# Weight squares of layer 1 taken during layer 0's merges, from a second load of each tile

## The chip, the cores and the metric

The kernel runs on one core of a Trainium2 chip. The metric is the device time of one execution in microseconds (us). The engines have their own instruction streams and meet by semaphores: TensorE (PE) multiplies matrices, VectorE (DVE), ScalarE (ACT) and GpSimd (POOL) work on tiles in on-chip memory, SyncE (SP) mostly issues loads. On each engine, and in SyncE's queue, instructions run in the order of the program.

## The reference

Two blocks run one after the other on 512 tokens of width 1024, in float32. The first (one layer: spatial gating, a sparse attention, a cross attention, a feed-forward part) is untouched. The second has two layers; each mixes 512 latent tokens and 256 context tokens by three branches (windowed attention a, latent attention b, gated convolution c), gates each branch's output and adds them up:

```
parts = split(h @ w_in, IN_SIZES)   # q,k,v; latents; conv b,c,u; z and g of each branch
ya, yb, yc = window_attention, latent_attention, gated_convolution
m = sigmoid(ga)*(ya @ w_branch[0]) + sigmoid(gb)*(yb @ w_branch[1]) + sigmoid(gc)*(yc @ w_branch[2])
x = x + gate * rms_norm(m @ w_o)
```

Layer 0 works on all 768 columns, layer 1 needs only the 512 latent ones at its end. `w_in` and `w_branch` differ by layer.

## The kernel before

Every float32 product is three float16 (or, for some weights, fp32r) matmuls of halves: hi x hi, lo x hi and hi x lo (lines 416 to 418). The weights' halves are made on the fly by the class `Stream`. It loads chunks of 128x1024 floats (512 KB) from SyncE's queue (line 205) into one of nine raw slots, in the order in which the products use them; makes a hi half `wh` on ScalarE (line 273) or, for convolution, latent and some gate weights, on GpSimd (line 271); and a lo half `wl` on VectorE (line 291, in pieces of 512 columns). Up to nine converted units stand in a ring ahead of TensorE. Once a chunk's lo half is made, its raw slot is free and `freed` issues the next load.

float16 halves need a scale. A group of chunks (the weights of one product, or of a gate and its branch) shares one, from the sum of all its squares. `stat` takes the squares of a raw chunk on ScalarE with a running sum along the row (line 224); the squared values go to the lo tile as scratch, and only the sum is kept. `scale` calls `total` (lines 427 to 433): a reduction on VectorE, a sum over the partitions on TensorE, a power on GpSimd, a reciprocal on VectorE. Only then can the group's halves be made. `stat` runs up to `AHEAD` = 4 chunks ahead of the conversion.

The scheduler of the framework fixes each engine's order before the launch, from its own times; the program only says in which order work is offered. The stage that matters are the twelve `merge` calls of each layer (three branches n, four column groups f2). A merge computes a gate tile (tanh on ScalarE, line 2129, named z) and a branch tile, and VectorE multiplies and adds them (lines 2133 to 2137). Products go through a pool of three PSUM tiles, `mm`. Behind the merges come the output product with `w_o` (fp32r, no squares), the residual chains (lines 2185 to 2206) with their norms, and the start of layer 1: keys and queries (L1556, L1586, L1589), whose transposed inputs are hTh and hTl (lines 421, 422), then attention with its probabilities P (line 721).

Of the kernel before, what the change touches and what calls it, by code (L numbers as in the profile page):

```python
# [9 lines left out]
FT = mybir.dt.float32  # L10
# [113 lines left out]
class Group:  # L124


    def __init__(self):
        self.total = self.seen = self.cols = 0
        self.t = None
        self.ready = False  # L130
        self.made = {}


class Blk:
# [42 lines left out]

G_S, G_I, G_C = 8, 9, 10  # L180


class Stream:
    def __init__(self, nc, slots, ringp, scalep, total, state, blks):
        self.nc, self.slots, self.ringp, self.scalep = nc, slots, ringp, scalep
        self.total, self.state = total, state
        self.chunks = [c for b in blks for c in b.chunks]
        self.units = []
        for ci, (_, us) in enumerate(self.chunks):
            for u in us:  # L190
                self.units.append((ci, u))
        self.raw = {}
        self.nd = 0
        self.ns = 0
        self.nstat = 0
        self.live = 0
        self.full = []
        self.half = None

    def loads(self):  # L200
        while self.nd < len(self.chunks) and self.slots:
# [7 lines left out]

    def stat(self, lo):  # L210
        nc = self.nc
        us = self.chunks[self.nstat][1]
        t = self.raw[self.nstat]
        self.nstat += 1
        g = us[0].blk.grp
        if g is None:
            return False
        if g.t is None:
            g.t = self.scalep.tile([128, 16], FT, tag="gs", name="gs")
        m = sum(len(u.ks) for u in us) * us[0].n  # L220
        w = lo.shape[-1]
        for a in range(0, m, w):
            b = min(m, a + w)
            nc.scalar.activation(lo[:, :b - a], t[:, a:b], AF.Square, accum_out=g.t[:, g.cols:g.cols + 1])  # L224
            g.cols += 1
        g.seen += 1
        if g.seen == g.total:
            self.full.append((self.state.clk, g))
        return True


    def scale(self):
        _, g = self.full.pop(0)
        self.total(g.t[:, 0:g.cols], g.t[:, G_S:G_S + 1], g.t[:, G_I:G_I + 1])
        g.ready = True

    def pump(self, must=False):
        self.loads()
        while self.full and self.full[0][0] + LAG <= self.state.clk:
            self.scale()  # L240
        if self.ns >= len(self.units) or self.live >= RING:
            self.finish()
            return False
        nc = self.nc
        ci, u = self.units[self.ns]
        t = self.raw[ci]
        fr = u.blk.fr
        g = u.blk.grp
        if not (must or fr or g.ready) and g.seen == g.total:
            return False  # L250
        hi, lo = (self.ringp.tile([128, 512 if fr else 1024], FR if fr else F16, tag=n, name=n) for n in ("wh", "wl"))
        if not fr:
            while g.seen < g.total:
                self.stat(lo)
            while not g.ready:
                self.scale()
        n = 1 if self.ns < 4 else 2
        while n and self.nstat < self.nd and self.nstat <= ci + AHEAD:
            n -= self.stat(lo)
        m = len(u.ks) * u.n  # L260
        src = t[:, u.off:u.off + m]
        self.finish()
        if u.blk.split is not None:
            u.blk.split(t, hi, lo)
        elif fr:
            nc.scalar.activation(hi[:, :m], src, AF.Copy)  # L266
            nc.vector.tensor_sub(lo[:, :m], src, hi[:, :m].bitcast(FT))  # L267
        else:
            s = g.t[:, G_S:G_S + 1]
            if u.blk.pool:  # L270
                nc.gpsimd.tensor_scalar(hi[:, :m], src, s, 1.0, op0=OP.mult, op1=OP.mult)  # L271
            else:
                nc.scalar.activation(hi[:, :m], src, AF.Copy, scale=s)  # L273
            self.half = lo[:, :m], src, s, hi[:, :m], ci, u
        u.hi, u.lo, u.split = hi, lo, True
        self.live += 1
        self.ns += 1
        if fr:
            u.ready = True
            if u.last:  # L280
                self.freed(ci)
        return True
# [10 lines left out]
            self.freed(ci)  # L293

    def freed(self, ci):
        self.slots.append(self.raw.pop(ci))
        self.loads()


    def unscale(self, blk, ih, mul=1.0):  # L300
        if blk.fr:
            return None
        while not blk.grp.ready:
            assert self.pump(True), "the weights cannot be read ahead"
        made = blk.grp.made
        key = id(ih), mul
        if key not in made:
            a = G_C + len(made)
            assert a < 16
            c = blk.grp.t[:, a:a + 1]  # L310
            self.nc.vector.tensor_scalar(c, blk.grp.t[:, G_I:G_I + 1], ih, mul, op0=OP.mult, op1=OP.mult)
            made[key] = c, ih
        return made[key][0]

# [17 lines left out]
def decoder_kernel(ctx: ExitStack, tc: tile.TileContext, A: dict, out: bass.AP):  # L332
# [14 lines left out]
    sp = pool("small", NS)  # L347
    s1p = pool("small2", NS2)
    dnp = pool("dn", 3)
    scalep = pool("scales", 12)  # L350
    sbp = pool("sb", 4)
    XN = lambda *a, **k: rot["xn"](*a, **k)
    Z = lambda *a, **k: rot["z"](*a, **k)
# [219 lines left out]
    H = {p: Halves(*[one.tile([128, 4, 512], FR, tag=f"H{p}{i}", name=f"hT{p}") for i in range(2)]) for p in "hl"}  # L573

    def hT16():
        for i, p in enumerate("hl"):
            H[p] = one.tile([128, 8, 512], F16, tag=f"H{p}0", name=f"hT{p}")
            more_raw(f"H{p}1")

    def more_raw(tag):  # L580
        t = one.tile([128, 2, 1024], FT, tag=tag, name="raw")
        stream.slots += [t[:, 0], t[:, 1]]
        stream.loads()
# [1649 lines left out]
    def layer(i):  # L2233
# [3 lines left out]
        every = [4, 5, 0, 1, 2, 3]  # L2237
        qt = every if i == 0 else [0, 1, 2, 3]
        nn = 768 if i == 0 else 512
        add(lambda: s23_start(i))  # L2240
        add(lambda b: form_a(b, every, hcx, ev_ka, f"l{i}"), wblk(w[:, KA:KA + 256]))
        add(lambda b: form_a(b, qt, hcx, ev_qa, f"l{i}", 0.125), wblk(w[:, QA:QA + 512]))
# [37 lines left out]
        for n, b in enumerate((2, 0, 1)):  # L2280
            if n == 0:
                add(lambda: yc_load(nn))
                for n2 in range(behind, len(pieces)):
                    f, sg = pieces[n2]
                    add(lambda *b, n2=n2: piece(n2), *([za[f]] if sg == segs[0] else []))
                add(lambda: ya_load(nn))
            elif n == 1:
                g = Group()
                for f2 in range(2):
                    add(lambda bl, f2=f2: zgate(f2, segs, bl, yb_d, nn),  # L2290
                        wblk(w[:, ZB + f2 * 256:ZB + (f2 + 1) * 256], g))
            for f2 in range(4):
                g = Group()
                add(lambda *bl, f2=f2, n=n, b=b: merge(f2, segs, bl, n == 0, n == 2, "cab"[n]),
                    wblk(w[:, GA + b * 1024 + f2 * 256:GA + b * 1024 + (f2 + 1) * 256], g),
                    wblk(A["w_branch_2"][i, b][:, f2 * 256:(f2 + 1) * 256], g))
        add(lambda: wo_start(i, nq))
        wo = A["w_o_2"][i]
        add(lambda b: form_a(b, qt, mA, wo0), wblk(wo[:, 0:512], fr=True))
# [145 lines left out]
```

## Time and profile before

| | |
|---|---|
| median of 3 runs | 2428.55 us (2423.89 to 2429.85) |
| profiled execution | 2421.47 us, span 2419.7 us |
| mean granted clock | 0.978 |
| TensorE busy | 2261.3 us, 93% of the span |
| VectorE, ScalarE, GpSimd | 1544.2, 1298.1, 320.7 us (64%, 54%, 13%) |
| loads and stores | 226.67 MB, mean 94 GB/s |
| squares, line 224 | 242, 222.9 us |

The profile is of one execution, the page's times add up to its span, and its time lies at the low end of the runs. Busy shares are averages over the whole span; the stretches of the table in the rows below differ a lot. Layer 0's merges run from about 1391 to 1565 us and beyond, with the output product behind them until about 1726; then the norms and the start of layer 1 until about 1770; layer 1's attention and convolution until about 2170; and its merges and output product to the end.

### The profile page before, as it was taken

The page shows a single profiled execution, that of the slowest core. Times are in us where ns is not written, and L with a number is a line of the kernel's source. Part 1 is how long each engine was busy: PE and PEld are TensorE (multiplying, and loading weights), DVE is VectorE, ACT ScalarE, POOL GpSimd, SP SyncE. Part 2 cuts the span into 40 slices and gives each one's busy share as a digit, 9 for nine tenths or more (in the row PEclk, how much of TensorE's full clock was granted, in tenths as well). Part 3 has the DMA queues.
Part 4 walks back from the last instruction along what each step waited for, and adds up shares of the span by engine and source line. Part 5 has one row for each costly group of instructions (what it writes and reads, how often), then busy time and mean ns, then how long its engine had stood idle before and what let it go on. Part 6 is the DMA issues. An engine that isn't in the chain of part 4 may idle for free. (4 is left out here: it accounts for less than half of the span.)

```text
span 2419.7 us, 38066 instructions
## 1 busy us (share of the span) xinstructions
PE 2261.3 (93%) x14342; PEld 1505.2 (62%) x14342; DVE 1544.2 (64%) x3136; ACT 1298.1 (54%) x2745; POOL 320.7 (13%) x703
## 2 busy tenths in 40 slices
PE   7899899899999989999988999999779999899998
PEld 6777687544444557767767566557546567764446
DVE  6878678656665677665777444443777657865543
ACT  5656457746655455535777434323535457775532
POOL 4320321100100211004000000000621121000001
PEclk9899899899999999999999999999989999999999
DMA  4512445534443411112221422211421113233311
GB/s 158 140 47 71 141 144 199 172 101 153 155 140 106 122 50 38 46 40 65 79 74 56 137 79 61 79 42 63 156 86 50 42 38 108 71 115 113 103 44 61
DMA packets 182220, 226.67 MB, mean 94 GB/s; under 512 B 28556, under 2 KB 130876, under 8 KB 182036
## 3 DMA queue, kind: packets, MB, share of 16 engines
q1 hardware_dynamic: 158084, 187.67, 25.1%
q10 hardware_dynamic: 23952, 36.57, 4.4%
q8 instruction: 112, 1.84, 0.3%
q14 instruction: 72, 0.59, 0.1%
HBM read 207.33 MB, written 16.88 MB: 93 GB/s over the span
## 5 line engine op out<-in xcount | busy, mean ns | idle before, releaser
L416 PE MATMUL mm<-hTh,wh 128*128 128x512 f16 (+1 forms) x1040 | 392.6, 378 | 7.3 <-ACT wh L273 3.1
L291 DVE SCALAR_TENSOR_TENSOR wl<-raw,gs,wh 128x512 f16<-128x512 f32 (+2 forms) x420 | 296.6, 751 | 150.6 <-ACT wl L224 116.5
L417 PE MATMUL mm<-hTl,wh 128*128 128x512 f16 (+1 forms) x1040 | 392.4, 377 | 0.0
L418 PE MATMUL mm<-hTh,wl 128*128 128x512 f16 (+1 forms) x1040 | 391.2, 377 | 0.0
L224 ACT ACTIVATE wl<-raw 128x1024 f16<-128x1024 f32 (+3 forms) x242 | 222.9, 921 | 69.6 <-PE mm L417 37.3
L416 PEld LDWEIGHTS <-wh 128*128 128x128 f16 x1712 | 168.0, 98 | 147.4 <-issue 6.8
L417 PEld LDWEIGHTS <-wh 128*128 128x128 f16 x1712 | 168.0, 98 | 146.1 <-issue 9.6
L418 PEld LDWEIGHTS <-wl 128*128 128x128 f16 x1712 | 167.8, 98 | 143.9 <-issue 0.6
L738 ACT ACTIVATE ph<-mm 128x512 f16<-128x512 f32 (+2 forms) x300 | 146.1, 502 | 162.4 <-PE mm L734 156.1
L273 ACT ACTIVATE wh<-raw,gs 128x1024 f16<-128x1024 f32 x156 | 175.3, 1141 | 105.9 <-PE mm L417 83.0
L266 ACT ACTIVATE wh<-raw 128x512 fp32r<-128x512 f32 (+2 forms) x244 | 141.7, 613 | 142.2 <-PE mm L418 49.7
L739 DVE SCALAR_TENSOR_TENSOR pl<-mm,ph 128x512 f16<-128x512 f32 (+2 forms) x300 | 165.9, 567 | 73.6 <-ACT ph L738 71.1
L267 DVE TENSOR_TENSOR wl<-raw,wh 128x512 fp32r<-128x512 f32 (+2 forms) x244 | 156.1, 667 | 55.3 <-ACT wh L266 40.2
L432 POOL TENSOR_TENSOR gs<-gs,nh 128x1 f32<-128x1 f32 x66 | 40.6, 616 | 1125.2 <-DVE gs L431 1079.3
L416 PE MATMUL mm<-wh,hTh 128*128 128x512 f32 (+5 forms) x512 | 181.7, 356 | 5.5 <-DVE vf L1589 2.0
L418 PE MATMUL mm<-wh,hTl 128*128 128x512 f32 (+5 forms) x512 | 180.1, 352 | 1.8 <-DVE hTl L422 1.7
L417 PE MATMUL mm<-wl,hTh 128*128 128x512 f32 (+5 forms) x512 | 180.1, 352 | 0.3 <-DVE wl L267 0.3
L734 PE MATMUL mm<-ident,P 128*128 128x128 f32 x928 | 153.9, 283 | 5.9 <-ACT P L721 2.0
L721 ACT ACTIVATE P<-S,s 128x768 f32<-128x768 f32 (+4 forms) x160 | 105.8, 666 | 35.1 <-PE mm L734 18.0
L734 PEld LDWEIGHTS mm<-ident,P 128*128 128x128 f32 x928 | 108.6, 145 | 19.6 <-ACT P L721 2.9
L2133 DVE SCALAR_TENSOR_TENSOR z<-z,mm 128x256 f32<-128x256 f32 (+1 forms) x72 | 42.8, 596 | 107.2 <-PE mm L418 98.9
L271 POOL TENSOR_SCALAR wh<-raw,gs 128x1024 f16<-128x1024 f32 (+3 forms) x54 | 65.8, 1219 | 328.2 <-PE mm L417 209.9
(503 smaller groups left out, 5360.8 us busy)
## 6 DMA issues: line engine op xcount, KB each, us to landing
raw<-in_w_in_dram SPq DMA_DIRECT2D x124, 512.0 KB, 3.5
raw<-in_w_ff_dram SPq DMA_DIRECT2D x64, 512.0 KB, 4.5
raw<-in_w_mod_dram SPq DMA_DIRECT2D x48, 512.0 KB, 5.1
raw<-in_w_branch_dram SPq DMA_DIRECT2D x24, 512.0 KB, 3.4
raw<-in_w_o_dram SPq DMA_DIRECT2D x16, 512.0 KB, 4.0
raw<-in_cmp_w_dram SPq DMA_DIRECT2D x16, 256.0 KB, 3.5
raw<-in_w_out_dram SPq DMA_DIRECT2D x8, 512.0 KB, 3.6
raw<-in_w_mkv_dram SPq DMA_DIRECT2D x8, 512.0 KB, 3.7
```

The source lines that it names most:

```text
L224: nc.scalar.activation(lo[:, :b - a], t[:, a:b], AF.Square, accum_out=g.t[:, g.cols:g.cols + 1])
L266: nc.scalar.activation(hi[:, :m], src, AF.Copy)
L267: nc.vector.tensor_sub(lo[:, :m], src, hi[:, :m].bitcast(FT))
L273: nc.scalar.activation(hi[:, :m], src, AF.Copy, scale=s)
L291: self.nc.vector.scalar_tensor_tensor(l[:, b], src[:, b], s, h[:, b], op0=OP.mult, op1=OP.subtract)
L416: PE.matmul(ps, ah, bh, start=start, stop=False)
L417: PE.matmul(ps, ah, bl, start=False, stop=False)
L418: PE.matmul(ps, al, bh, start=False, stop=stop)
L721: ACT.activation(P, v[:, j, :], AF.Exp, bias=it.nb[:, j:j + 1], accum_out=it.den[:, j:j + 1])
L734: PE.transpose(ps[:, a - a0, :], it.P[0 if len(it.P) == 1 else j][:, c:c + 128], ident)
L738: ACT.activation(ph[:, :m], ps[:, :m], AF.Copy, scale=PSC)
L739: DVE.scalar_tensor_tensor(pl[:, :m], ps[:, :m], PSC, ph[:, :m], op0=OP.mult, op1=OP.subtract)
```

## The change

At layer 0's merge (n = 0, f2 = 1) the next raw slot that comes free is kept (`keep`, `slot`) and not given back to the stream. From then on, each time the stream is pumped, `early_step` may issue one extra load of a chunk of layer 1 into that slot (line 263), and the step after it takes the chunk's squares in place on ScalarE (line 276), with the sums in a small tile `gse` of 14 groups. When all are done the slot goes back. The 39 chunks are layer 1's first key and query weights (2 and 4), convolution (16), latent (3 and 4) and za gate weights (4), and the weights of its first two merges (6): some 20 MB loaded twice. The regular load of each stays; its squares (line 224, now 234) don't: `stat` passes over the chunks in `seen`. On ScalarE 49 squares of layer 1 (22 of 1024 columns, 20 of 512, 7 between) give way to 39 in layer 0's merges. The pool of scale tiles goes from 12 buffers to 6. Until the first early load each engine has the same instructions in the same order.

```diff
--- before.py
+++ after.py
@@ -129,6 +129,7 @@
         self.t = None
         self.ready = False
         self.made = {}
+        self.at = 8, 9, 10, 16
 
 
 class Blk:
@@ -177,7 +178,8 @@
 
 
 
-G_S, G_I, G_C = 8, 9, 10
+
+EARLY = 4, 5, 6, 8
 
 
 class Stream:
@@ -196,6 +198,10 @@
         self.live = 0
         self.full = []
         self.half = None
+        self.index = {id(c): i for i, c in enumerate(self.chunks)}
+        self.jobs, self.job, self.seen = [], None, set()
+        self.every = self.next = 0.0
+        self.slot, self.keep = None, False
 
     def loads(self):
         while self.nd < len(self.chunks) and self.slots:
@@ -209,12 +215,16 @@
 
     def stat(self, lo):
         nc = self.nc
-        us = self.chunks[self.nstat][1]
-        t = self.raw[self.nstat]
+        i = self.nstat
+        us = self.chunks[i][1]
+        t = self.raw[i]
         self.nstat += 1
         g = us[0].blk.grp
-        if g is None:
+        if g is None or i in self.seen:
             return False
+        if i == self.job:
+            self.early_sum()
+            return True
         if g.t is None:
             g.t = self.scalep.tile([128, 16], FT, tag="gs", name="gs")
         m = sum(len(u.ks) for u in us) * us[0].n
@@ -223,19 +233,67 @@
             b = min(m, a + w)
             nc.scalar.activation(lo[:, :b - a], t[:, a:b], AF.Square, accum_out=g.t[:, g.cols:g.cols + 1])
             g.cols += 1
+        g.cols -= 1
+        self.counted(g)
+        return True
+
+
+    def early(self, blks, tile, every):
+        grps = []
+        for b in blks:
+            if b.grp not in grps:
+                grps.append(b.grp)
+            self.jobs += [self.index[id(c)] for c in b.chunks]
+        n = EARLY[3]
+        for i, g in enumerate(grps):
+            assert g.t is None
+            g.t, g.at = tile[:, i * n:(i + 1) * n], EARLY
+        self.every, self.next = every, self.state.clk
+        self.keep = True
+
+    def early_step(self):
+        if self.slot is None or self.state.clk < self.next:
+            return
+        if self.job is not None:
+            self.early_sum()
+        while self.jobs:
+            i = self.jobs.pop(0)
+            if i >= self.nd:
+                for dst, src in self.chunks[i][0]:
+                    self.nc.sync.dma_start(out=dst(self.slot), in_=src)
+                self.job = i
+                break
+        if self.job is None:
+            self.slots.append(self.slot)
+            self.slot = None
+        self.next = self.state.clk + self.every
+
+    def early_sum(self):
+        us = self.chunks[self.job][1]
+        g = us[0].blk.grp
+        m = sum(len(u.ks) for u in us) * us[0].n
+        t = self.slot[:, :m]
+        self.nc.scalar.activation(t, t, AF.Square, accum_out=g.t[:, g.cols:g.cols + 1])
+        self.seen.add(self.job)
+        self.job = None
+        self.counted(g)
+
+    def counted(self, g):
+        g.cols += 1
         g.seen += 1
         if g.seen == g.total:
             self.full.append((self.state.clk, g))
-        return True
 
 
     def scale(self):
         _, g = self.full.pop(0)
-        self.total(g.t[:, 0:g.cols], g.t[:, G_S:G_S + 1], g.t[:, G_I:G_I + 1])
+        a = g.at
+        self.total(g.t[:, 0:g.cols], g.t[:, a[0]:a[0] + 1], g.t[:, a[1]:a[1] + 1])
         g.ready = True
 
     def pump(self, must=False):
         self.loads()
+        self.early_step()
         while self.full and self.full[0][0] + LAG <= self.state.clk:
             self.scale()
         if self.ns >= len(self.units) or self.live >= RING:
@@ -266,7 +324,7 @@
             nc.scalar.activation(hi[:, :m], src, AF.Copy)
             nc.vector.tensor_sub(lo[:, :m], src, hi[:, :m].bitcast(FT))
         else:
-            s = g.t[:, G_S:G_S + 1]
+            s = g.t[:, g.at[0]:g.at[0] + 1]
             if u.blk.pool:
                 nc.gpsimd.tensor_scalar(hi[:, :m], src, s, 1.0, op0=OP.mult, op1=OP.mult)
             else:
@@ -293,8 +351,12 @@
             self.freed(ci)
 
     def freed(self, ci):
-        self.slots.append(self.raw.pop(ci))
-        self.loads()
+        t = self.raw.pop(ci)
+        if self.keep:
+            self.slot, self.keep = t, False
+        else:
+            self.slots.append(t)
+            self.loads()
 
 
     def unscale(self, blk, ih, mul=1.0):
@@ -305,10 +367,11 @@
         made = blk.grp.made
         key = id(ih), mul
         if key not in made:
-            a = G_C + len(made)
-            assert a < 16
+            g = blk.grp
+            a = g.at[2] + len(made)
+            assert a < g.at[3]
             c = blk.grp.t[:, a:a + 1]
-            self.nc.vector.tensor_scalar(c, blk.grp.t[:, G_I:G_I + 1], ih, mul, op0=OP.mult, op1=OP.mult)
+            self.nc.vector.tensor_scalar(c, g.t[:, g.at[1]:g.at[1] + 1], ih, mul, op0=OP.mult, op1=OP.mult)
             made[key] = c, ih
         return made[key][0]
 
@@ -347,7 +410,7 @@
     sp = pool("small", NS)
     s1p = pool("small2", NS2)
     dnp = pool("dn", 3)
-    scalep = pool("scales", 12)
+    scalep = pool("scales", 6)
     sbp = pool("sb", 4)
     XN = lambda *a, **k: rot["xn"](*a, **k)
     Z = lambda *a, **k: rot["z"](*a, **k)
@@ -573,9 +636,12 @@
     H = {p: Halves(*[one.tile([128, 4, 512], FR, tag=f"H{p}{i}", name=f"hT{p}") for i in range(2)]) for p in "hl"}
 
     def hT16():
-        for i, p in enumerate("hl"):
+        for p in "hl":
             H[p] = one.tile([128, 8, 512], F16, tag=f"H{p}0", name=f"hT{p}")
             more_raw(f"H{p}1")
+
+    early = {}
+    gse = one.tile([128, 14 * EARLY[3]], FT, tag="gse", name="gse")
 
     def more_raw(tag):
         t = one.tile([128, 2, 1024], FT, tag=tag, name="raw")
@@ -2237,6 +2303,7 @@
         every = [4, 5, 0, 1, 2, 3]
         qt = every if i == 0 else [0, 1, 2, 3]
         nn = 768 if i == 0 else 512
+        n0 = len(ops)
         add(lambda: s23_start(i))
         add(lambda b: form_a(b, every, hcx, ev_ka, f"l{i}"), wblk(w[:, KA:KA + 256]))
         add(lambda b: form_a(b, qt, hcx, ev_qa, f"l{i}", 0.125), wblk(w[:, QA:QA + 512]))
@@ -2294,6 +2361,10 @@
                 add(lambda *bl, f2=f2, n=n, b=b: merge(f2, segs, bl, n == 0, n == 2, "cab"[n]),
                     wblk(w[:, GA + b * 1024 + f2 * 256:GA + b * 1024 + (f2 + 1) * 256], g),
                     wblk(A["w_branch_2"][i, b][:, f2 * 256:(f2 + 1) * 256], g))
+                if i == 0 and (n, f2) == (0, 1):
+                    add(lambda: stream.early(early[1], gse, 8000))
+                elif (n, f2) == (0, 1):
+                    early[i] = [b for blks, _ in ops[n0:] for b in blks if not b.fr]
         add(lambda: wo_start(i, nq))
         wo = A["w_o_2"][i]
         add(lambda b: form_a(b, qt, mA, wo0), wblk(wo[:, 0:512], fr=True))
```

The places where instructions move are shown as they stand in each engine's order. In the changed kernel's numbering, 211 is the regular load, 234 the regular square, 331 the hi half, 349 the lo half, 263 and 276 the early load and square; 2195 is the merge's z, 484 and 485 are hTh and hTl. A name's number (raw_155) is only an instance.

ScalarE in the merges, before:

```order
1471 L2129 ACTIVATE z_17210<-mm_17175,gs_16396 128x256
1472 L2129 ACTIVATE z_17253<-mm_17228,gs_16396 128x512
1473 L2129 ACTIVATE z_17295<-mm_17270,gs_16396 128x256
1474 L273 ACTIVATE wh_17325<-raw_5953,gs_16970 128x1024
1475 L224 ACTIVATE wl_17326,gs_17169<-raw_153 128x1024
1476 L273 ACTIVATE wh_17344<-raw_5053,gs_16970 128x1024
1477 L224 ACTIVATE wl_17345,gs_17169<-raw_5049 128x1024
1478 L2129 ACTIVATE z_17348<-mm_17312,gs_16396 128x512
```

The same place after, with the last early squares:

```order
1500 L2195 ACTIVATE z_17275<-mm_17238,gs_16425 128x256
1501 L276 ACTIVATE raw_5054,gse_126<-raw_5054 128x1024 x2
1502 L2195 ACTIVATE z_17325<-mm_17293,gs_16425 128x512
1503 L276 ACTIVATE raw_5054,gse_126<-raw_5054 128x1024
1504 L2195 ACTIVATE z_17369<-mm_17344,gs_16425 128x256
1505 L276 ACTIVATE raw_5054,gse_126<-raw_5054 128x1024
1506 L331 ACTIVATE wh_17399<-raw_155,gs_17027 128x1024
1507 L234 ACTIVATE wl_17400,gs_17232<-raw_5050 128x1024
1508 L276 ACTIVATE raw_5054,gse_126<-raw_5054 128x1024
1509 L331 ACTIVATE wh_17420<-raw_156,gs_17027 128x1024
1510 L234 ACTIVATE wl_17421,gs_17232<-raw_5954 128x1024
1511 L2195 ACTIVATE z_17424<-mm_17386,gs_16425 128x512
```

One or two early squares stand between two evacuations z; the last of the 39 is row 1508, and the z of row 1511 is that of row 1478 before. The first of them is row 1397 there, behind the z of row 1396, which is row 1396 before.

SyncE's queue at the same stage, before:

```order
244 L205 DMA raw_5049<-in_w_in_2_dram 128x4x256
245 L205 DMA raw_5053<-in_w_in_2_dram 128x4x256
246 L205 DMA raw_5953<-in_w_branch_2_dram 128x4x256
247 L205 DMA raw_5953<-in_w_in_2_dram 128x4x256
248 L205 DMA raw_5053<-in_w_in_2_dram 128x4x256
249 L205 DMA raw_154<-in_w_branch_2_dram 128x4x256
```

After:

```order
244 L211 DMA raw_5050<-in_w_in_2_dram 128x4x256
245 L263 DMA raw_5054<-in_w_in_2_dram 128x4x256 x2
246 L263 DMA raw_5054<-in_w_in_2_dram 128x2x512 x3
247 L211 DMA raw_5954<-in_w_in_2_dram 128x4x256
248 L263 DMA raw_5054<-in_w_in_2_dram 128x2x512
249 L211 DMA raw_5954<-in_w_branch_2_dram 128x4x256
250 L263 DMA raw_5054<-in_w_in_2_dram 128x4x256
251 L211 DMA raw_5054<-in_w_in_2_dram 128x4x256
252 L263 DMA raw_5054<-in_w_in_2_dram 128x4x256 x4
253 L211 DMA raw_155<-in_w_in_2_dram 128x4x256
```

The first early load has the place of the regular load of row 245; from there on regular loads, 19 until the last early one, stand in the queue behind early loads, each of which waits for the square before it.

VectorE at the start of layer 1, before (hTl is the first transposed input of its keys):

```order
2043 L291 SCALAR_TENSOR_TENSOR wl_18900<-raw_154,gs_18756,wh_18899 128x512 x2
2044 L291 SCALAR_TENSOR_TENSOR wl_18776<-raw_5953,gs_18344,wh_18775 128x512 x2
2045 L311 TENSOR_SCALAR gs_18756<-gs_18756,ih_5710 128x1
2046 L291 SCALAR_TENSOR_TENSOR wl_18831<-raw_5053,gs_18344,wh_18830 128x512 x2
2047 L2196 SCALAR_TENSOR_TENSOR xt_18619<-ob_18163,s2_18796,xt_18619 128x512
2048 L2199 SCALAR_TENSOR_TENSOR xt_18619<-z_18785,s2_18796,xt_18619 128x512
2049 L422 TENSOR_TENSOR hTl_5052<-S_18917,hTh_5048 128x4x128
```

After:

```order
2079 L349 SCALAR_TENSOR_TENSOR wl_18879<-raw_156,gse_126,wh_18878 128x512 x2
2080 L349 SCALAR_TENSOR_TENSOR wl_18888<-raw_154,gse_126,wh_18887 128x512 x2
2081 L349 SCALAR_TENSOR_TENSOR wl_18897<-raw_5050,gse_126,wh_18896 128x512 x2
2082 L349 SCALAR_TENSOR_TENSOR wl_18930<-raw_5050,gse_126,wh_18929 128x512 x2
2083 L349 SCALAR_TENSOR_TENSOR wl_18939<-raw_5954,gse_126,wh_18938 128x512 x2
2084 L349 SCALAR_TENSOR_TENSOR wl_18948<-raw_5954,gse_126,wh_18947 128x512
2085 L485 TENSOR_TENSOR hc_8118<-S_18811,hc_8118 128x4x128
2086 L349 SCALAR_TENSOR_TENSOR wl_18948<-raw_5954,gse_126,wh_18947 128x512
2087 L485 TENSOR_TENSOR hTl_5053<-S_18904,hTh_5049 128x4x128
```

The lo halves of layer 1's first weights now stand ahead of the input hTl; before, some of them stood behind it.

## Rows read from the trace of the kernel before

**Rows 1.** Stretches: length, busy of PE, PEld, DVE, ACT, POOL; clock, DMA share, GB/s.

```profile
1391.00:1565.00 174.00, 174.00 (x1079) 104.78 (x1078) 73.94 (x153) 75.19 (x123) 4.40 (x8) 1.00 0.22 68
1565.00:1726.00 161.00, 161.00 (x880) 111.57 (x878) 69.14 (x111) 50.63 (x98) 19.22 (x48) 1.00 0.22 73
1726.00:1770.00 44.00, 21.51 (x162) 17.48 (x160) 36.45 (x71) 23.84 (x56) 21.39 (x37) 0.81 0.54 173
1770.00:1830.00 60.00, 50.96 (x296) 30.92 (x297) 44.28 (x98) 27.03 (x55) 12.25 (x11) 0.94 0.19 56
1830.00:2000.00 170.00, 160.54 (x1158) 105.41 (x1157) 114.06 (x300) 83.20 (x221) 35.75 (x71) 1.00 0.16 46
2000.00:2170.00 170.00, 154.15 (x1121) 120.35 (x1120) 129.08 (x258) 125.53 (x281) 9.47 (x20) 0.98 0.30 94
2170.00:2400.00 230.00, 230.00 (x1068) 116.44 (x1067) 117.46 (x217) 104.58 (x163) 8.71 (x18) 1.00 0.25 78
```

**Rows 2.** The squares of line 224 (ns min/median/max, first and last start, forms).

```profile
L224 ACT ACTIVATE wl<-raw x242: 612/1040/1064, 443.9 to 2303.9; 128x1024 f16<-128x1024 f32 x83, 128x512 fp32r<-128x512 f32 x31, 128x768 f16<-128x768 f32 x4, 128x864 f16<-128x864 f32 x2
```

**Rows 3.** The loads into raw slots from 1380 to 1600 us.

```profile
DMA to landing us min/median/max: 3.3/3.4/3.6
```

**Rows 4.** SyncE's timeline (start, length, instruction, [idle before <- what ended it]).

```profile
1393.62 3.01 SPq L205 DMA_DIRECT2D raw<-in_w_in_dram  x2
...
1396.27 0.37 SPq L205 DMA_DIRECT2D raw<-in_w_in_dram  x1
...
1741.09 0.37 SPq L205 DMA_DIRECT2D raw<-in_w_in_dram  x1
```

**Rows 5.** ScalarE's timeline, at three places.

```profile
1388.44 1.04 ACT L224 ACTIVATE wl<-raw 128x1024 f16<-128x1024 f32 x1
1389.39 0.19 ACT L224 ACTIVATION_READ_ACCUMULATOR wl<-raw 128x1 f32 x1
...
1561.78 1.15 ACT L273 ACTIVATE wh<-raw,gs 128x1024 f16<-128x1024 f32 x1 [0.38 <-PE mm L417]
...
1563.88 0.67 ACT L2129 ACTIVATE z<-mm,gs 128x512 f32<-128x512 f32 x1
...
1744.58 1.06 ACT L224 ACTIVATE wl<-raw 128x1024 f16<-128x1024 f32 x1 [1.47 <-DMA raw<-in_w_in_dram]
```

**Rows 6.** VectorE's timeline, at two places.

```profile
1392.14 1.41 DVE L291 SCALAR_TENSOR_TENSOR wl<-raw,gs,wh 128x512 f16<-128x512 f32 x2 [1.11 <-ACT wl L224]
...
1741.55 6.57 DVE L291 SCALAR_TENSOR_TENSOR wl<-raw,gs,wh 128x512 f16<-128x512 f32 x6
```

**Rows 7.** TensorE's timeline in the merges: first matmuls of three tiles.

```profile
1561.74 0.38 PE L416 MATMUL mm<-yal,wh 128*128 128x512 f16 x1
...
1564.33 0.27 PE L416 MATMUL mm<-hc,wh 128*128 128x256 f16 x1
...
1566.95 0.27 PE L416 MATMUL mm<-yhl,wh 128*128 128x256 f16 x1
```

**Rows 8.** What TensorE waited for, 1715 to 1780 us (total, times, longest).

```profile
PE S L1581 <- ACT kd L1556: 8.6, 1, 8.6
PE S L630 <- DVE hTl L422: 5.7, 1, 5.7
```

**Rows 9.** The same, 1780 to 1830 us, then 2000 to 2170 us.

```profile
PE S L1632 <- ACT P L721: 5.1, 1, 5.1
...
PE S L416 <- ACT P L721: 6.9, 10, 1.1
```

**Rows 10.** GpSimd's timeline beside the six lo halves.

```profile
1741.59 4.67 POOL L271 TENSOR_SCALAR wh<-raw,gs 128x1024 f16<-128x1024 f32 x3
```

**Rows 11.** TensorE behind two gaps, and the stretch behind the first.

```profile
1813.47 0.58 PE L1632 MATMUL S<-k,q 128*128 128x256 f32 x1 [5.06 <-ACT P L721]
...
1919.81 0.39 PE L1632 MATMUL S<-k,q 128*128 128x256 f32 x1 [2.48 <-ACT P L721]
...
1813.00:1816.00 3.00, 2.53 (x12) 2.44 (x13) 0.85 (x2) 1.37 (x5) 0.00 (x0) 0.50 0.23 83
```

## The prediction, written before the changed kernel was run

> **What bounds the kernel now.** I read the table of stretches first, since the change touches two stages with different limits. From 1391 to 1726 us, the merges of layer 0 and the output product behind them, TensorE is busy in every one of the 174.00 and 161.00 us, at a granted clock of 1.00, and ScalarE in 75.19 of the first 174.00 [rows 1]. So in the merges ScalarE and the queues have room, but a delay of TensorE adds to the time, and nothing up to 1726 gives it back. From 1726 to 2170 us TensorE stands for 44.00 - 21.51 = 22.5, then 9.0, 9.5 and 15.9 us, 57 in all [rows 1]. What layer 1's squares cost can only lie in there. From 2170 on TensorE is full again.
>
> Next the row of the squares: 242 of them, 1040 ns at the median [rows 2], each with a read of its sum of 0.19 us [rows 5]. 49 of the 242 belong to this change. Last come TensorE's waits in the 57 us, which say what was late [rows 8, 9].
>
> **What it adds: a chain of 39 links.** A second load of a tile goes from SyncE's queue into the one slot kept for it, ScalarE squares it there, and only then may the next load issue. From trace rows one link is:
> - Issue to square. A load issued at 1741.09 is squared from 1744.58, with ScalarE idle for 1.47 us before it, until the data came: 3.49 us [rows 4, 5]. The load itself lands after 3.3/3.4/3.6 us (min/median/max of the loads in the merges) [rows 3].
> - The square and the read of its sum: 1388.44 to 1389.39 + 0.19 = 1389.58, so 1.14 us [rows 5].
> - From the engine's end to the waiting load. A lo half ends at 1392.14 + 1.41 = 1393.55 and the load into its slot issues at 1393.62: 0.07 us [rows 4, 6].
>
> 3.49 + 1.14 + 0.07 = 4.70 us. Seven tiles are narrower than 1024 columns; their squares save about 0.2 each. 38 steps come to 38 x 4.70 - 1.4 = 177.2 us. The first early load stands where the queue issued a load at 1396.27 [rows 4], so the first square starts at 1399.8 and the last at 1577.0.
>
> Where must it be? In ScalarE's new order the last square stands just ahead of the hi conversion that ran at 1561.78 [rows 5]: 162.0 us behind the first, 4.26 us a link. So it comes 15.2 us too late. Behind it on ScalarE are this conversion, one regular square and the gate's evacuation z, which then starts about 2.1 us after that conversion, as before (1563.88 - 1561.78), hence at 1577.0 + 1.14 + 2.1 = 1580.2. The product tiles have three buffers: the gate tile is done at 1561.74, the branch tile fills until 1564.33, the next gate tile until 1566.95, and the branch matmul at 1566.95 needs the first one back [rows 7]. z takes 0.67, so it may start up to 1566.3: TensorE is held for 1580.2 - 1566.3 = 13.9 us, in many small gaps.
>
> Two things are not in this. Some 19 regular loads stand between the early ones on the same queue, and a regular load ahead of an early one shares the transfer: nothing to 0.6 us each (1393.62 and 1396.27 are 2.65 apart, less than a landing [rows 3, 4]), so 0 to 11 us; most issue while the slot is being squared, and I take 2. One raw slot less (8 for 9) and the regular loads queued behind a waiting early one: the loads' share is 0.22 there [rows 1], and the converted units run several chunks ahead of TensorE, so nothing. The loss is then 13.9 + 2 = 16 us. Bounds: if the links hold at the 4.26 us of the order, 0; with every extra 16 + 9 = 25. Below nothing is excluded: TensorE has no idle time in this stage to win.
>
> Here the Trainium skill speaks against my link ("DMA: Bandwidth & Descriptors", section "Anatomy of one DMA — SWDGE (gpsimd) path"): about 2.0 us fixed plus bytes over 436 GB/s. For 512 KB that is 3.2 us, an estimate from that page; its fit is for another issuing path than SyncE's queue. By it a link would be some 0.2 us shorter and the loss about 8 us instead of 16. The trace has 3.3 as its lowest landing and 3.49 to the square's start [rows 3 to 5], and these decide.
>
> **What it removes.** 49 squares leave ScalarE in layer 1, 22 of full size at 1.04, 20 of half size at 0.61, 7 between at some 0.85, and 49 reads at 0.19 [rows 2, 5]: 50 us of work, of which only what lay before a TensorE wait counts:
> - 1726 to 1770: TensorE waited 8.6 us for kd and 5.7 for hTl [rows 8]. A square stood there for 1.47 us, waiting for its load, and took 1.14 [rows 5], and the next did the like: 5.2 us of ScalarE ahead of kd. But VectorE is busy for 36.45 of the 44 us [rows 1], and its lo halves stay: 16 before, 16 after, 13 of which now go ahead of the first hTl. One group of six took 6.57 us where two take 1.41, beside hi conversions on GpSimd [rows 6, 10]. Weights that are ready earlier let the halves fill VectorE's 7.6 idle us. Gain 0 to 8.6, and down to -3 if hTl merely waits behind the halves; I take 4.
> - 1770 to 1830: 5.1 us for the probabilities P [rows 9], four squares on ScalarE nearby (4 x 1.14 = 4.6). 0 to 5; I take 1, since VectorE is again the busier (44.28 of 60).
> - 1830 to 2000: seven squares, 9.5 us idle in many small waits. 0 to 4; 1.
> - 2000 to 2170: ten products waited 6.9 us in all for ScalarE's P [rows 9], which is busy 125.53 of 170 us [rows 1]; ten half squares go (10 x 0.80 = 8 us). 0 to 6.9; 2.
>
> Sum: 8 us, bounds -3 and 24. The group sums and their reciprocals move with the squares and are as many; fewer buffers for scales add waits on GpSimd for work long done: nothing.
>
> **Sum.** +16 - 8 = +8 us. On the profiled execution (2421.47, 1.8 more than its span of 2419.7) that is 2429.5. That execution lies 7.1 us below the median of the runs, 2428.55, and the change is counted from the median: 2436.5, rounded to 2436.
>
> **Rivals.**
> - The chain keeps pace, and layer 1 pays. For it: ScalarE is busy for under half of the merges, the loads' share is 0.22, and a link has only to be 4.3 us; the earlier transfers of a link may overlap. Against: 3.49 us from issue to square, twice alike, and z behind each square. Loss 0 to 2, gain 8 to 10: 2420.5.
> - The two cancel, either because the link is nearer to 4.5 us (38 x 0.2 = 7.6 us less), or because layer 1's waits for P and kd go with the squares. Loss 8, gain 8: 2428.5, no change. It is also where the removal does not bring what it says: with the squares gone, the lo halves on VectorE are late next, the gain is 0 to 2 and the loss must be small too.
> - The other end: the clock. In layer 1 a gap of 5.06 us before the matmul at 1813.47 left it at 0.58 us, against 0.39 after a gap of 2.48, and the stretch 1813 to 1816 has a granted clock of 0.50, the lower of the two levels, 1.2 of 2.4 GHz [rows 11]. If the chain holds z in gaps of about 5 us, the merges' matmuls run at half speed behind each, for at least the 2.5 us that those rows show, 1.3 us lost a gap. Eight gaps cost 10 us; with the forecast's 16, half of the other bound's 9, and 7 gained: about +24, 2452. It decides as soon as two squares with late loads stand between two evacuations. Against: the order mostly has an evacuation after one or two squares, and the gaps are spread.
>
> **How the numbers follow.** A measurement of this kernel tells about 0.3%, 7 us, from no change. The forecast (+2 to +16 us) has 0.40, the chain that keeps pace 0.18, cancelling 0.28, the clock 0.14. Slower by over 0.3%: 0.30 of the forecast's, all of the clock's, and some of the second's edge: 0.48. Faster: 0.15 of the first rival and 0.04 of the second's edge: 0.19. The rest, 0.33, is within. The range runs from the first rival's 2420 to the clock's 2452; the likeliest case's own is 2430 to 2445.
>
> **What would show it.** Right: between 1396 and about 1580 us TensorE stands for 10 to 20 us, waiting for z or for the mm buffers behind it; ScalarE's idle time in front of the early squares ends with the early load, with 3.4 to 3.6 us from issue to square; links of 4.6 to 4.8 us; 1726 to 2170 (shifted) shorter by 5 to 12 us, with VectorE next in the transition. Wrong: TensorE full in the merges; or links under 4.3 us; or the transition longer, hTl standing behind the lo halves; or a stretch of the merges with a granted clock under 0.9.

## The result, and the profile after

| | before | after |
|---|---|---|
| median of 4 runs each | 2426.22 us | 2449.05 us |
| ratio to before, 95% interval | | 1.0098 [1.0083, 1.0113] |
| profiled execution's span | 2419.7 us | 2445.8 us |
| mean granted clock | 0.978 | 0.972 |

The change makes the kernel slower by 22.8 us. The forecast had +8 us and a range up to 2452: the side is right, the time lies in the range, and the size is a third of what was measured.

The table of stretches after the change, with ends put at the same matmuls as the first five stretches of [rows 1] (columns as there):

```profile
1392.00:1766.00 374.00, 347.46 (x1955) 218.04 (x1954) 151.49 (x319) 156.40 (x277) 29.87 (x70) 0.96 0.39 116
1766.00:1807.30 41.30, 26.62 (x174) 20.34 (x172) 34.45 (x65) 17.79 (x43) 19.39 (x35) 0.79 0.56 180
1807.30:1868.60 61.30, 53.26 (x294) 32.11 (x295) 43.83 (x91) 18.76 (x39) 11.93 (x9) 0.92 0.20 54
1868.60:2032.70 164.10, 158.99 (x1155) 105.70 (x1153) 111.98 (x274) 73.39 (x198) 32.73 (x71) 1.00 0.17 47
2032.70:2195.90 163.20, 150.06 (x1117) 116.83 (x1115) 126.47 (x240) 117.17 (x256) 5.13 (x11) 1.00 0.32 95
```

The first row stands for two rows of before, 174.00 + 161.00 = 335 us, in which TensorE never stood: now it is 374.00 - 347.46 = 26.5 us idle, and busy for 12.5 us more with the same matmuls, at a granted clock of 0.96. That is +39.0. The other rows, against 44.00, 60.00, 170.00 and 170.00, give -2.7, +1.3, -5.9 and -6.8: layer 1 gives 14 us back. Both terms of the forecast are there, and both are larger.

Two evacuations z bound the loss. One stands ahead of the first early square, the other behind the last, of a tile that TensorE has just finished in both. Before:

```profile
1395.34 0.47 ACT L2129 ACTIVATE z<-mm,gs 128x256 f32<-128x256 f32 x1 [0.58 <-PE mm L418]
...
1620.46 0.69 ACT L2129 ACTIVATE z<-mm,gs 128x512 f32<-128x512 f32 x1 [5.29 <-PE mm L418]
```

After:

```profile
1396.34 0.47 ACT L2195 ACTIVATE z<-mm,gs 128x256 f32<-128x256 f32 x1 [0.58 <-PE mm L481]
...
1661.81 0.69 ACT L2195 ACTIVATE z<-mm,gs 128x512 f32<-128x512 f32 x1 [5.28 <-PE mm L481]
```

So the merges lose 41.35 - 1.0 = 40.3 us. What TensorE waited for from 1390 to 1640 us (total, times, longest):

```profile
PE mm L479 <- ACT z L2195: 20.4, 7, 4.0
PE S L493 <- DVE sb L491: 4.8, 2, 4.5
PE mm L479 <- DVE z L1779: 1.4, 1, 1.4
```

Nearly all is TensorE's wait for z. The second row is a group's sum, one matmul in TensorE's order that waits for a regular square behind early ones on ScalarE. The line of the early squares and the idle time of ScalarE in front of them:

```profile
L276 ACT ACTIVATE raw<-raw x39: 682/1056/1057, 1401.0 to 1601.5; 128x1024 f32<-128x1024 f32 x32, 128x768 f32<-128x768 f32 x4, 128x864 f32<-128x864 f32 x2, 128x576 f32<-128x576 f32 x1
...
  DMA raw<-in_w_in_dram: 88.3, 30
  DMA raw<-in_w_branch_dram: 4.8, 2
```

The landing that the profile gives for the loads of line 263 is

```profile
DMA to landing us min/median/max: 3.4/3.5/3.7
```

but it is known for only 4 of the 39, none of them a late one.

The chain lasts 200.5 us and not 177.2. The timelines show three kinds of link. Of the plain kind:

```profile
1405.97 1.06 ACT L276 ACTIVATE raw<-raw 128x1024 f32<-128x1024 f32 x1 [2.43 <-DMA raw<-in_w_in_dram]
1406.93 0.19 ACT L276 ACTIVATION_READ_ACCUMULATOR raw<-raw 128x1 f32 x1
1410.79 1.06 ACT L276 ACTIVATE raw<-raw 128x1024 f32<-128x1024 f32 x1 [3.67 <-DMA raw<-in_w_in_dram]
```

ScalarE stands for 3.67 us until the tile is there, and the link is 4.82. Of the second kind, in which ScalarE is busy with other work when the tile lands:

```profile
1486.29 1.06 ACT L276 ACTIVATE raw<-raw 128x1024 f32<-128x1024 f32 x1 [2.64 <-DMA raw<-in_w_in_dram]
...
1487.74 1.13 ACT L331 ACTIVATE wh<-raw,gs 128x1024 f16<-128x1024 f32 x1
1488.78 1.04 ACT L234 ACTIVATE wl<-raw 128x1024 f16<-128x1024 f32 x1
...
1489.82 1.13 ACT L331 ACTIVATE wh<-raw,gs 128x1024 f16<-128x1024 f32 x1
1490.86 1.04 ACT L234 ACTIVATE wl<-raw 128x1024 f16<-128x1024 f32 x1
...
1491.90 0.67 ACT L1778 ACTIVATE z<-mm,gs 128x512 f32<-128x512 f32 x1
1492.47 1.04 ACT L276 ACTIVATE raw<-raw 128x1024 f32<-128x1024 f32 x1
```

SyncE issues this load at 1487.46, and it is there at 1491.0; but two hi halves, two regular squares and a z stand ahead of its square in ScalarE's order. The link is 6.18 us. Of the third kind, ScalarE and SyncE's queue:

```profile
1473.67 1.04 ACT L276 ACTIVATE raw<-raw 128x1024 f32<-128x1024 f32 x1
...
1481.53 1.06 ACT L276 ACTIVATE raw<-raw 128x1024 f32<-128x1024 f32 x1 [3.51 <-DMA raw<-in_w_in_dram]
...
1472.64 0.37 SPq L211 DMA_DIRECT2D raw<-in_w_in_dram  x1
1474.71 0.37 SPq L211 DMA_DIRECT2D raw<-in_w_branch_dram  x1
1475.18 12.65 SPq L263 DMA_DIRECT2D raw<-in_w_in_dram  x3
```

Here ScalarE waits for the tile, and the tile is late: the early load issues at 1475.18, behind two regular loads (the last row joins it with the two after it), and its square starts 6.35 us later. The link is 7.86 us.

Of the 38 links, from the starts of the 39 squares, 24 take 4.69 us on average, against 177.2 / 38 = 4.66 as priced, and 14 take 6.28: 14 x 1.62 = 22.7 us that the sum did not have. The table of ScalarE's idle time tells the 14 apart, since 32 of the 39 squares waited for their load and 7 did not. Those 7 are of the second kind: six stood behind a block of two hi halves, two squares and a z of some 5 us, and one behind the halves yhl. They took 9.9 us more than priced. The other 7 waited for a load that took 4.0 to 6.3 us from issue to square. In five of them two regular loads had been issued in the 3 us before it, in one a regular load 1.3 us before, in one a regular load 0.4 us behind it; no plain link had two regular loads so near. They took 12.7 us more than priced; at most 0.7 us of a link passed before the issue, while SyncE issued a regular load.

TensorE's delay shows in two forms, gaps and a lower clock. TensorE's timeline at three of the gaps, and behind the second of them:

```profile
1491.48 0.16 PE L493 MATMUL S<-sb,onesb 128*128 128x1 bf16 x1 [4.51 <-DVE sb L491]
...
1545.74 0.27 PE L479 MATMUL mm<-yal,wh 128*128 128x256 f16 x1 [3.70 <-ACT z L2195]
...
1549.02 0.63 PE L481 MATMUL mm<-hTh,wl 128*128 128x512 f16 x1
...
1549.87 0.38 PE L480 MATMUL mm<-hTl,wh 128*128 128x512 f16 x1
...
1605.36 0.37 PE L479 MATMUL mm<-yhl,wh 128*128 128x256 f16 x1 [3.68 <-ACT z L2195]
```

and the table of three stretches there:

```profile
1546.50:1549.80 3.30, 3.11 (x12) 1.64 (x12) 2.65 (x6) 2.46 (x5) 0.00 (x0) 0.50 0.86 271
1491.90:1498.60 6.70, 4.58 (x11) 1.62 (x11) 4.05 (x12) 2.79 (x7) 0.55 (x1) 0.50 0.81 235
1604.50:1611.30 6.80, 5.95 (x22) 3.04 (x22) 5.94 (x22) 2.20 (x5) 1.15 (x2) 0.50 0.85 273
```

The granted clock is 0.50 there, the lower level of 1.2 GHz, behind gaps of 3.70, 4.51 and 3.68 us. The 26.5 us of gaps and the 12.5 us of slower work are not a sum on top of the chain's lateness: the last early square is 200.5 - 162.0 = 38.5 us late by the distance of the prediction, which by itself comes near the 40.3 us that the merges lost. No run isolates what the lower clock added. It plainly adds behind the last gap, where no early square follows: an estimate from the last row is half of 5.95, some 3 us.

### The profile page after: what moved, and what is told of

The parts are those of the page before. It is cut to its first block, busy times and chain, and to the rows that moved or that the text cites. A ratio compares the mean times of both kernels' runs of the same rounds, so it can differ in the third digit from the quotient of the medians.

```text
span 2445.8 us, 38140 instructions
## 1 busy us (share of the span) xinstructions
PE 2276.9 (93%) x14342; PEld 1507.6 (62%) x14342; DVE 1545.7 (63%) x3136; ACT 1296.2 (53%) x2725; POOL 317.2 (13%) x703
## 5 line engine op out<-in xcount | busy, mean ns | idle before, releaser
L479 PE MATMUL mm<-hTh,wh 128*128 128x512 f16 (+1 forms) x1040 | 395.9, 381 | 10.7 <-ACT z L2195 5.3
L349 DVE SCALAR_TENSOR_TENSOR wl<-raw,gs,wh 128x512 f16<-128x512 f32 x342 | 239.9, 747 | 155.8 <-ACT wl L234 128.5
L234 ACT ACTIVATE wl<-raw 128x1024 f16<-128x1024 f32 (+3 forms) x193 | 181.4, 940 | 54.3 <-PE mm L480 36.0
L331 ACT ACTIVATE wh<-raw,gs 128x1024 f16<-128x1024 f32 x144 | 161.6, 1139 | 79.5 <-PE mm L480 57.9
L495 POOL TENSOR_TENSOR gs<-gs,nh 128x1 f32<-128x1 f32 x52 | 30.3, 583 | 894.9 <-DVE gs L494 818.8
L771 DVE TENSOR_REDUCE s<-S 128x1 f32<-128x768 f32 (+4 forms) x112 | 97.6, 875 | 16.5 <-PE S L481 10.0
```

The lines of the kernel that those rows point to most:

```text
L349: self.nc.vector.scalar_tensor_tensor(l[:, b], src[:, b], s, h[:, b], op0=OP.mult, op1=OP.subtract)
L479: PE.matmul(ps, ah, bh, start=start, stop=False)
```

## The experiments

The theory: ScalarE, in its fixed order, stands for each early load; links that follow one another without slack add up their lateness, z comes late, TensorE stops. The rivals: ScalarE's 45 us of added work in the merges; or the second load's traffic and its place in SyncE's queue. The edits are shown in part, against the changed kernel; `...` marks what is left out.

**Neither loads nor squares**

```diff
-                for dst, src in self.chunks[i][0]:
-                    self.nc.sync.dma_start(out=dst(self.slot), in_=src)
...
-        self.nc.scalar.activation(t, t, AF.Square, accum_out=g.t[:, g.cols:g.cols + 1])
...
+    nc.vector.memset(gse, 1.0)
```

> Leaves out both the early loads and the early squares: the sums of the 14 groups are a constant, so layer 1's first groups are scaled by a constant and have no squares anywhere. It measures what layer 1 gains by itself. Theory (the loss of 40 us lies in layer 0's merges, where ScalarE waits in its order for each early load, and layer 1 gives 15 back): about 2411 us, TensorE full from 1391 to 1726. Rival (layer 1's gain of 15 us in the changed kernel only makes up for waits that the late merges had caused): about 2426, as before.

Measured 2410.46 us, ratio 0.9941 [0.9918, 0.9964]; TensorE busy in all 335.00 us from 1391 to 1726. Layer 1 gains some 14 us by itself, so what it gave back is not an echo of the late merges.

**Squares without loads**

```diff
-                for dst, src in self.chunks[i][0]:
-                    self.nc.sync.dma_start(out=dst(self.slot), in_=src)
...
-        self.nc.scalar.activation(t, t, AF.Square, accum_out=g.t[:, g.cols:g.cols + 1])
+        self.nc.scalar.activation(t, t, AF.Abs, accum_out=g.t[:, g.cols:g.cols + 1])
```

> Leaves out the early loads: the 39 passes with a running sum stay on ScalarE, over what happens to lie in the kept slot (absolute values in place of squares). Theory (ScalarE's waits for the loads cost the time, not its work): within 5 us of the kernel without both, about 2411 to 2416. Rival (45 us of added ScalarE work in the merges holds the evacuations): at least 2435.

Measured 2412.81 us, 0.9948 [0.9930, 0.9966], not told apart from the last. The merges' stretch:

```profile
1391.00:1600.00 209.00, 208.58 (x1295) 125.46 (x1294) 94.54 (x213) 126.23 (x214) 8.60 (x15) 1.00 0.24 71
```

ScalarE is busy for 126.23 us, more than the 110.17 in the same stretch of the changed kernel, and TensorE misses 0.42. By itself ScalarE's added work is not the cost. With no loads the order packs these passes closer (up to six between two z), so the test is of the work, not of the places.

**Loads without squares**

```diff
-        self.nc.scalar.activation(t, t, AF.Square, accum_out=g.t[:, g.cols:g.cols + 1])
...
+    nc.vector.memset(gse, 1.0)
```

> Leaves out the early squares, keeps the 39 early loads in the one slot, each behind the one before; the sums are a constant. Nothing on ScalarE waits for them. Theory (ScalarE's waits): 2411 to 2416. Rival (the 20 MB, the queue and the missing slot make regular weights late): at least 2435, with TensorE waiting for hi and lo halves in the merges.

Measured 2427.87 us, 1.0010 [0.9997, 1.0023]: 17 us above the kernel without both, and neither theory's number. TensorE's one long wait and what is behind it on ScalarE:

```profile
1538.95 0.37 PE L478 MATMUL mm<-yal,wh 128*128 128x256 f16 x1 [13.04 <-ACT z L2195]
```

```profile
1537.18 1.06 ACT L234 ACTIVATE wl<-raw 128x1024 f16<-128x1024 f32 x1 [15.51 <-DMA raw<-in_w_branch_dram]
```

This regular square waited 15.51 us for a regular load, which SyncE issued at 1531.91, behind early loads that each waited for the one before. So my theory missed a second form of the same thing: in SyncE's order a regular load can be late behind a chain. In the changed kernel no regular square waited for its load, so there this form cost nothing that the waits show; there, seven early loads that issued beside regular ones came late.

**Two slots**

```diff
-        if self.keep:
-            self.slot, self.keep = t, False
+        if self.keep:            # keep = 2
+            self.two.append((t, None))
+            self.keep -= 1
...
```

with the square of one slot taken while the other's load is under way.

> Keeps two of the nine raw slots, so that the next early load is under way while a tile is squared. Theory in its first form (the serial chain through one slot is what is long): ScalarE finds its tiles landed, the merges lose under 10 us, 2411 to 2421. In its second form (the fixed order puts each square at a point where its load has not landed yet, with one slot or with two): the order packs the squares closer, ScalarE still waits for most of them, and the time stays at 2436 to 2455.

Measured 2432.74 us, 1.0025 [1.0014, 1.0036]: between the two forms, nearer to the second. The squares now run from 1402.5 to 1528.2; idle time before them:

```profile
  DMA raw<-in_w_in_dram: 38.8, 18
  DMA raw<-in_w_branch_dram: 5.3, 2
```

ScalarE finds half of its tiles landed and still stands for the other half: the squares now follow one another by (1528.2 - 1402.5) / 38 = 3.3 us on average. TensorE's waits for z and the group's sum fall to 10.9 and 4.0 us.

**One slot, 29 tiles**

```diff
-                    early[i] = [b for blks, _ in ops[n0:] for b in blks if not b.fr]
+                    early[i] = [b for blks, _ in ops[n0:] for b in blks if not b.fr][:12]
```

> The changed kernel with 29 of the 39 tiles: the za gate weights and the first two merges of layer 1 keep their late squares. Theory (ScalarE, in its order, waits for the load of each link; the loss is per link): the merges lose 40 x 29/39 = 30 us, layer 1 gives back 10 to 14, 2441 to 2446. Rival (the loss comes from a few places, the tail of the chain or the groups' scale sums in TensorE's order): 2425 to 2435.

Measured 2439.02 us, 1.0070 [1.0044, 1.0096]. The time is a little under the theory's and above the rival's. The waits fall to 10.8 (z) and 3.6 us (sum): the loss grows with the length of the chain, though not in proportion.

**29 tiles, by freed slots**

```diff
     def freed(self, ci):
         t = self.raw.pop(ci)
...
+        if self.job is not None:
+            self.early_sum()
+            self.slots.append(self.slot)
+            self.loads()
+        while self.jobs and self.job is None:
+            i = self.jobs.pop(0)
+            if i >= self.nd:
+                self.slot, self.job = t, i
+                for dst, src in self.chunks[i][0]:
+                    self.nc.sync.dma_start(out=dst(t), in_=src)
+                return
...
```

`early_step` does nothing here, and the list of tiles is cut to 29 as in the run before.

> The same 29 tiles, but no slot is kept: each raw slot that a conversion frees takes an early load first and a regular load after its square, so the early loads are some 8 us apart, set by TensorE and not by the chain. Theory: ScalarE waits under 1 us a tile, the merges lose under 5 us, 2412 to 2420. Rival (early loads and squares in the merges cost whatever their distance): 2435 to 2446, as with one slot.

Measured 2415.67 us, 0.9965 [0.9952, 0.9978], 23 us under the same 29 tiles in one slot; TensorE is busy in all 335.00 us. This is the run that decides: the same loads and squares, without a kept slot and in other places.

**All 39, by freed slots**

The edit of the last run, with the whole list of tiles.

> All 39 tiles by freed slots. The last ten or so squares then fall into the output product and the norms behind it. Theory: no loss in the merges, but these squares meet the norms that bound the start of layer 1, so no better than with 29: 2413 to 2425. Rival (each square moved out of layer 1 pays the same): 5 us better than with 29.

Measured 2411.28 us, 0.9948 [0.9930, 0.9966]. It is 4.4 us under the 29 and below the theory's 2413 to 2425: the rival's number, though the intervals overlap. The squares behind the merges (the last at 1744.5) cost nothing that can be seen. The table, and ScalarE's idle time before the squares:

```profile
1391.00:1726.00 335.00, 335.00 (x1956) 213.31 (x1955) 150.05 (x313) 154.83 (x268) 27.92 (x65) 1.00 0.39 122
```

```profile
L277 ACT ACTIVATE raw<-raw x39: 685/1057/1062, 1403.4 to 1744.5; 128x1024 f32<-128x1024 f32 x32, 128x768 f32<-128x768 f32 x4, 128x864 f32<-128x864 f32 x2, 128x576 f32<-128x576 f32 x1
...
  DMA raw<-in_w_in_dram: 40.5, 22
```

"Under 1 us a tile" was wrong: ScalarE stands 40.5 / 22 = 1.8 us where it waits. It costs nothing that TensorE shows. The reason is read from the order and not tested by itself: a slot comes free only when TensorE has used what was converted before, so the squares are (1744.5 - 1403.4) / 38 = 9.0 us apart on average, and ScalarE catches up between them. A wait in order is harmless while its lateness isn't handed to the next.

**Early loads from ScalarE's queue**

```diff
-                    self.nc.sync.dma_start(out=dst(self.slot), in_=src)
+                    self.nc.scalar.dma_start(out=dst(self.slot), in_=src)
```

> The changed kernel with the early loads issued from ScalarE's queue, right behind the square before; SyncE's queue holds the regular loads alone. Theory (ScalarE's wait in its order for each tile): the merges lose about as much, 2440 to 2455. Rival (the loss is that of regular loads queued behind early ones): at most 2430.

Measured 2441.82 us, 1.0066 [1.0043, 1.0090], as the theory has it. ScalarE's idle time before the squares is 78.1 us in 30 places, for 93.1 in 32. The two evacuations that bound the loss:

```profile
1400.07 0.47 ACT L2195 ACTIVATE z<-mm,gs 128x256 f32<-128x256 f32 x1 [0.58 <-PE mm L481]
...
1654.84 0.69 ACT L2195 ACTIVATE z<-mm,gs 128x512 f32<-128x512 f32 x1 [5.29 <-PE mm L481]
```

Between them 254.77 - 225.12 = 29.7 us are lost, for 40.3. So SyncE's queue has a share in the loss, 7 us by the medians and 10.7 by these two executions, and most of it stays without it. Late loads stay too:

```profile
1423.25 0.37 SPq L211 DMA_DIRECT2D raw<-in_w_in_dram  x1
1425.33 0.37 SPq L211 DMA_DIRECT2D raw<-in_w_branch_dram  x1
...
1425.46 0.38 ACTq L263 DMA_DIRECT2D raw<-in_w_in_dram  x1
...
1430.72 1.06 ACT L276 ACTIVATE raw<-raw 128x1024 f32<-128x1024 f32 x1 [2.85 <-DMA raw<-in_w_in_dram]
```

This load, on another queue than the two regular ones just before it, takes 5.26 us to its square. So the place in SyncE's queue alone does not make a load late; what is common to both runs is that several transfers are under way together. One gap of TensorE in this run, and the stretch behind it:

```profile
1571.85 0.27 PE L479 MATMUL mm<-yal,wh 128*128 128x256 f16 x1 [3.66 <-ACT z L2195]
...
1571.85:1575.25 3.40, 3.30 (x23) 2.14 (x23) 3.37 (x8) 3.40 (x6) 0.00 (x0) 1.00 0.59 209
```

The granted clock is 1.00 behind this gap of 3.66 us.

**All 39, by freed slots, from one merge earlier**

```diff
-                if i == 0 and (n, f2) == (0, 1):
+                if i == 0 and (n, f2) == (0, 0):
```

Everything else as in the run with all 39 by freed slots.

> All 39 tiles by freed slots, begun one merge earlier (three freed slots sooner), so that three fewer squares fall behind the merges. Theory (squares beside the norms of layer 1's start cost a little, those in the merges nothing): 1 to 3 us under the version begun at the second merge, 2408 to 2411. Rival (they cost nothing there either): the same 2411, within 1 us.

Measured 2410.57 us, 0.9934 [0.9917, 0.9951]: it beats both kernels, as the other two by freed slots do, and lies 16 us under before. From the one begun later it is not told apart, nor from the kernel without loads and squares, and both expected numbers fit it.

## Why the prediction was wrong

- What bounds the kernel: right. The merges have no slack on TensorE, and the delay stayed.
- The link of 4.70 us: right for 24 of 38. By the Trainium skill ("DMA: Bandwidth & Descriptors", section "Anatomy of one DMA — SWDGE (gpsimd) path") the link would have been 0.2 shorter, an estimate; the 3.4 to 3.7 us to landing, known for four of these loads, say no.
- **The failed step** is "38 steps come to 38 x 4.70 - 1.4 = 177.2 us", with the 2 us taken for shared transfers. The chain took 200.5 us. Two terms were mis-sized. First, the sum lets every square start when its tile lands. I had read ScalarE's share of the merges, under a half, as room, but its conversions stand in blocks of some 5 us, and 7 links stood behind such work: 9.9 us where the sum has nothing. Second, regular loads beside an early one were priced at "nothing to 0.6 us each", 11 us at most, and I took 2: seven late loads cost 12.7 us. The landing of 3.3 to 3.6 us [rows 3] is known for only 4 of the 28 loads of its stretch, so it could not show this. So the last square was 200.5 - 162.0 = 38.5 us late, against 15.2 forecast, and the merges lost 40.3 us, against 16 with an upper bound of 25.
- The missing slot: no regular square waited for its load, so it cost nothing that the waits show.
- The half clock was held apart as a rival with a condition that failed: I asked for gaps of about 5 us, from a gap of 5.06 with it and one of 2.48 without it [rows 11]. Gaps of 3.68 and 3.70 us had it too. One of 3.66 us, in the run on ScalarE's queue, did not. So the length of a gap alone does not tell. The sign of being wrong, a stretch of the merges with a granted clock under 0.9, came. That the rival's time, 2452, came nearest is partly chance: it had the half clock right, at 10 us, and the chain not.
- The gain: 8 forecast, 14 measured twice. The start of layer 1 gave 2.7 of the 4: the wait for kd fell from 8.6 to 0.2 us, but one of 8.0 us that ends with hc on VectorE came in its place. The next stretch lost 1.3 where a gain of 1 was expected; VectorE stays the busier there, 43.83 of 61.30 us. The two long stretches gave 5.9 and 6.8 in place of 1 and 2. TensorE's waits for P account for 3.6 of these 12.7 us (from 4.3 and 6.9 to 1.9 and 5.7), and the clock of 0.98 from 2000 to 2170 [rows 1], which is 1.00 now, for some 3.4 (170 x 0.02, an estimate). Where the rest comes from stays open.
- The rival in which the chain keeps pace needed links of 4.3 us; the shortest of full size took 4.57. With paced slots its time, 2420.5, is even undercut.

## What to carry to other kernels

An instruction that waits for a load in an engine's fixed order holds everything behind it. Price a serial chain of load and use by the load's landing, beside the other loads that are under way, plus all that stands on that engine between two links, and compare it with the distance that the order leaves; spare time as a share of the stretch does not answer that. Such work is best tied to an event that the bounding engine paces, here a slot freed by TensorE's progress: the same loads and squares then went from +23 to -13 us.

## What was not expected of the hardware

- Gaps of 3.68 and 3.70 us on TensorE were followed by a granted clock of 0.50, with 128x512 matmuls at 0.63 us in place of 0.38; one of 3.66 us in another run was followed by 1.00.
- An early load that issued within 3 us behind two regular ones took 4.7 to 6.3 us to its square, against 3.4 to 3.8 us in most plain links. One that came from another queue took 5.26 us.
